# A hybrid decoder layer on one core: what GpSimd did before the MLP goes to VectorE, ScalarE and TensorE

## The chip, the core and the metric

The kernel runs on one core of one Trainium2 chip. The metric is the device time of one execution in microseconds. Five engines work side by side on the core: TensorE (PE in the profile, its weight loads PEld), VectorE (DVE), ScalarE (ACT), GpSimd (POOL) and SyncE (SP), which here only issues the DMAs. Each runs its own instructions in order and waits on semaphores for the others.

## The reference

One layer of a decoder trunk on a residual stream x of 1024 positions by 1024 features, in float32, with a conditioning vector c:

```
mod = silu(c) @ w_mod + b_mod                  # shift, scale, gate for mixer and MLP: 6 x 1024
h = rms(x, norm1_w) * (1 + sc1) + sh1
u, q, k, v = split(h @ w_in)                   # 512 | 512 | 128 | 128
y_ssm  = S5(u): 32 groups of 16 channels, each driving a 64-dim complex diagonal state,
         scan over 1024 positions, y = Re(C s) + D u, z = gelu(y), z * sigmoid(z @ w_glu + b_glu)
y_attn = attention: 8 query heads, 2 key/value heads, window 128, per-head rms of q and k,
         relative bias, sinks
x = x + g1 * (concat(rms(y_ssm), rms(y_attn)) @ w_out)
h2 = rms(x, norm2_w) * (1 + sc2) + sh2
x = x + g2 * ((silu(gate) * val) @ w_down),  [val | gate] = causal_conv3(h2 @ w_up)
```

## The kernel before

Everything lies transposed: features on the 128 partitions, positions along the free dimension, in pieces of 128x512 (half a row of positions, called h = 0 and 1) or 128x1024. Every float32 product is made of three matmuls in a reduced format (`mm3`): each operand is split into a high part, a cast, and a low part, source minus high part (`split`, the cast by `hi_eng`, the subtraction by `lo_eng`). The subtraction and all other two-operand elementwise work goes through the helper `tt(eng, ...)` on line 127, so that VectorE's and GpSimd's share of it have the same line; `cpy` on lines 142 and 144 makes casts and copies. Which engine does which is written in the table `PICK`, one letter for each use (a ScalarE, v VectorE, p GpSimd), read by `pick(name, i)`.

The stages, in order of the program:

1. First projection. For k = 0 to 7 a tile of x (128 features by 1024 positions), a column block of w_mod and half a block of w_in are loaded. `emit_mod` makes one column of mod on VectorE, x times its scale is split into `hT[k]` (hi on ScalarE L261, lo on VectorE), x squared on ScalarE (L265), and the squares are added up in `acc`, by GpSimd from k = 1 on. TensorE adds up the projection U in six banks (j = 0 to 5: every eighth position) as the k come, and j = 6 and 7 beside or after that. From `acc` eight matmuls give the row sums in columns (`rc`, which scales U when it leaves its bank), and two more the sums in rows (`rstd`).
2. Tables. Small VectorE operations on 128x32 (exp, sin, powers `PWr`, `PWi`) give the discretised state matrix; `outer` makes four tiles `IB` and five tiles `CAt` of 128x1024 from them, three elementwise operations each, taken in turn by GpSimd and VectorE.
3. Heads and scan. The order of TensorE's instructions is pinned to the order of the program here. `head(t)` projects k, v and four pairs of q; the SSM inputs `SR` and `SI` are made on TensorE and scanned in twelve steps of `cmac` (six up, six down). Each step multiplies and adds in eight operations on n columns of each of the 16 pairs of groups; the first `SCAN_CUT` of the 16 go to VectorE, with the product in PSUM, the rest to GpSimd.
4. Attention in 16 units (8 blocks of 128 queries, 2 key/value heads), at high priority, beside the SSM's output, GELU and GLU. GpSimd scales most units' softmax by its row sum (`PM`).
5. Norms of the two branches, output projection. For the SSM branch the norm factor `rss` is not in the operand: `proj` multiplies it in when a bank is emptied (VectorE, into `xs_`), and GpSimd adds the result to x (`XA`). For the attention branch VectorE adds straight to x. Sums of squares for the second norm follow (`R`, `RA`).
6. MLP with a seven-product scheme (`product`, `weight`, `took`, `operands`, `mixed`), convolution and down projection. Some of its splits are GpSimd's, before and after the change.

The order on every engine inside a stretch that is not pinned comes from a planner in the framework, which orders the instructions by a model of their times when the program is built. A tag such as X4 or A8 is a buffer; the next use of a tag waits for the last reader. All DMAs are issued from SP's one queue, in order.

Of the kernel before, what the change touches and what calls it, by code (L numbers as in the profile page):

```python
# [27 lines left out]
for _n, _w in (  # L28
# [19 lines left out]
}  # L48

SCAN_CUT = (12, 14, 8, 9, 11, 13, 9, 8, 11, 11, 12, 9)  # L50
# [21 lines left out]
def hymba_kernel(ctx, tc, xT, c, wmod, wu, wkvq, small, consts, relb, pq, wglu, wout, wup, wdn, out):  # L72
# [173 lines left out]
    acc = new("A2")  # L246
    xs = [new("X4"), new("X5"), new("X6"), early[:, 3072:4096]]
    wst = None
    for k in range(8):
        xk = xs[k % 4]  # L250
        sync.dma_start(out=xk, in_=xT[k])
        emit_mod(8 + k, early[:, (k % 3) * 1024:(k % 3 + 1) * 1024], cact)
        if k % 2 == 0:
            wst = new(("W0", "A10")[k // 2 % 2])
            sync.dma_start(out=wst, in_=wu[k // 2])
        w = half(newr(f"U{k}") if k < 4 else wux[:, (k - 4) * 1024:(k - 3) * 1024])
        wus.append(w)
        split(w, wst[:, (k % 2) * 512:(k % 2) * 512 + 512], "a", pick("WL", k))
# [20 lines left out]
    rc = pool.tile([128, 16], F32, name="rc")  # L279
# [139 lines left out]
    tt(pol, gh(Bb), gh(Q1), bg(fr), MUL)  # L419
    tt(pol, gh(jt), gh(Q2), bg(t0), MUL)  # L420
    tt(pol, Bb, Bb, jt, ADD)
    tt(pol, gh(Bsw), gh(Q2), bg(f2), MUL)
    tt(pol, gh(jt), gh(Q1), bg(t2), MUL)
    tt(pol, Bsw, Bsw, jt, ADD)
    tt(pol, P1, P1, S("sgn").to_broadcast([128, 512]), MUL)
    tt(pol, P2, P2, S("neg").to_broadcast([128, 512]), MUL)
# [45 lines left out]
    def head_w(t):  # L472
# [3 lines left out]
        split(w, wst, pick("HWH", t), pick("HWL", t))  # L476
# [195 lines left out]
    sgi = [0]  # L672
    ptmp = CAt[4][:, 576:1024]

    def cmac(l, dst, src, n):
        GP = SCAN_CUT[sgi[0]]
        sgi[0] += 1
        step = max(1, 512 // n)
        cuts = [(vec, g0, min(GP, g0 + step)) for g0 in range(0, GP, step)]
        step = max(1, 448 // n)  # L680
        cuts += [(pol, g0, min(16, g0 + step)) for g0 in range(GP, 16, step)]
        for eng, g0, g1 in cuts:
            shp = [128, g1 - g0, n]
            tp = (bank[7] if eng is vec else ptmp)[:, 0:(g1 - g0) * n].rearrange("p (g c) -> p g c", c=n)
# [19 lines left out]
    for h in range(2):  # L704
        for i in range(4):
            q_ = newr(f"H{8 + 4 * h + i}")
            for kv in range(2):
# [4 lines left out]
                cpy(pick("QH%d" % h, i), q.r[p0, :], src)  # L712
                tt(ENG[pick("QL%d" % h, i)], q.r[p1, :], src, q.f[p0, :], SUB)
# [49 lines left out]
    for h in range(2):  # L763
        for m in range(4):
            zs[m, h] = half(newr(f"A{m + 4 * h}"))
            split(zs[m, h], zT[m][:, h * 512:h * 512 + 512], pick("ZH", m), pick("ZL", m))
    wg = []
    wgt = (newr("HA"), newr("HB"))
    for k in range(4):
# [4 lines left out]
        split(wg[k], wst[:, (k % 2) * 512:(k % 2) * 512 + 512], pick("GH", k), pick("GL", k))  # L774
# [4 lines left out]
    rss = half(new("W1"))  # L779
# [3 lines left out]
    for h in range(2):  # L783
# [8 lines left out]
        acc, sq = half(new(("A8", "A8")[h]))  # L792
        for n in range(4):
            hi, lo = mx[n, h] = half(newr(f"A{n + 4 * h}"))
            src = zT[n][:, hs]
            if pick("MX%d" % h, n) == "a":
                act.activation(out=hi.r, in_=src, func=AF.Identity, scale=bw[:, n:n + 1])
            else:
                ts(hi.r, src, bw[:, n:n + 1], MUL)
            stt(lo.r, src, bw[:, n:n + 1], hi.f, MUL, SUB)  # L800
            if pick("NS0%d" % h, n) == "a":
                act.activation(out=(sq if n else acc), in_=src, func=AF.Square)
            else:
                tt(ENG[pick("NS0%d" % h, n)], (sq if n else acc), src, src, MUL)
            if n:
                tt(ENG[pick("NA0%d" % h, n - 1)], acc, acc, sq, ADD)
        b = sbank()
        pe.matmul(b, ones, acc, start=True, stop=True)
        rsqrt_mean(rss[h], sq, b, 2048)


    def branch_norm(h):
# [4 lines left out]
        for m in range(1, 4):  # L817
            if pick("NS1%d" % h, m - 1) == "a":
                act.activation(out=sq, in_=src[m], func=AF.Square)
            else:  # L820
                tt(ENG[pick("NS1%d" % h, m - 1)], sq, src[m], src[m], MUL)
            tt(ENG[pick("NA1%d" % h, m - 1)], acc, acc, sq, ADD)
# [3 lines left out]
        for m in range(4):  # L826
# [3 lines left out]
            split(mx[4 + m, h], yo, pick("MH1%d" % h, m), pick("ML1%d" % h, m))  # L830
# [65 lines left out]
    def wload(src, lo_eng=None):  # L896
# [5 lines left out]
        split(w, st, pick("LH", i), lo_eng or "p")  # L902
# [6 lines left out]
    def proj(d, h, br_i, b, w):  # L909
# [11 lines left out]
    xs_ = half(new("A8"))  # L921
# [6 lines left out]
    for i, d in enumerate(order):  # L928
        if i % 2 == 0:
# [4 lines left out]
            split(w, st, pick("SH", i // 2), pick("SL", i // 2))  # L934
# [25 lines left out]
    def normed(k, h, rs):  # L960
        t_ = ht[k, h]
        stt(t_, x[k][:, h * 512:h * 512 + 512], mods[:, 8 + k:9 + k], rs, MUL, MUL)
        if pick("HB", 8 * h + k) == "a":
            act.activation(out=t_, in_=t_, func=AF.Identity, bias=mod[:, 24 + k:25 + k])
        else:
            ts(t_, t_, mod[:, 24 + k:25 + k], ADD)
# [55 lines left out]
    def attn_out(d, h):  # L1022
# [4 lines left out]
        if d % 2 == 0:  # L1027
            accs["w"] = wload(wo2[1, :, d:d + 2], pick("AL%d" % h, d // 2))
# [4 lines left out]
        else:  # L1033
            sq = ((sq,) + tuple(spare[h]))[d % 3]
            e_ = pick("R%d" % h, d)
            if e_ == "a":
                act.activation(out=sq, in_=x[d][:, hs], func=AF.Square)
            else:
                tt(ENG[e_], sq, x[d][:, hs], x[d][:, hs], MUL)
            tt(ENG[pick("RA%d" % h, d)], acc, acc, sq, ADD)  # L1040
# [361 lines left out]
```

## Time and profile before

| what | us |
|---|---|
| three runs, median (lowest to highest) | 1176.59 (1175.77 to 1176.9) |
| the profiled execution, its own time | 1173.97 |
| its span, first to last instruction | 1172.2 |

The span is what the views below divide up; the profiled execution's own time is 1.8 us longer. The granted clock of TensorE is 0.949 of full speed over the span. A busy time is the union of the instructions of an engine; neighbours on one engine overlap by some 0.08 us in the records. In the views, an arrow `out<-in` names tiles without their numbers (tX stands for X4 to X7, bk for a PSUM bank, tS for the tile S16). In brackets behind a row is the idle time before it, with what ended it.

### The profile page before, as it was taken

Reading aid. Unit: us, or ns where it says so; the run is one execution under the profiler, and the core shown is the slowest. Engines: PE = TensorE matmul, PEld = TensorE weight load, DVE = VectorE, ACT = ScalarE, POOL = GpSimd, SP = SyncE. Lnnn points to the kernel's source line nnn. Section 1 sums busy time; section 2 is a strip of 40 time slices with the busy share of each in tenths; the row PEclk is TensorE's granted clock in tenths of the full one; section 3 lists DMA queues with packets and bytes.
Section 4 is the critical chain, followed back from the end, with each engine's and each line's share of the span. In section 5 each row is a group of like instructions: output and inputs, shape, how many; then the busy total and the mean of one; then the engine's idle time right before and its main releaser. Section 6 shows DMA issues by size and latency. Waiting matters only on the chain.

```text
span 1172.2 us, 13402 instructions
## 1 busy us (share of the span) xinstructions
PE 1047.8 (89%) x4664; PEld 827.1 (71%) x4664; DVE 997.3 (85%) x1493; ACT 523.9 (45%) x889; POOL 500.7 (43%) x344
## 2 busy tenths in 40 slices
PE   4757989777989788869999999999999979989998
PEld 4646867565656466647888888888888758768777
DVE  8999799988989988698787788878796797997985
ACT  4312232163676234565555454545454455434442
POOL 3674276636266772684222222212122043343551
PEclk9778999978999899889999999999999989999999
DMA  9402330605322633323222333242222439320002
GB/s 355 151 27 72 63 100 19 90 1 146 124 108 106 200 126 123 130 91 107 76 94 101 113 103 114 103 144 73 90 90 72 162 132 406 126 91 1 1 37 107
DMA packets 47334, 128.13 MB, mean 109 GB/s; under 512 B 6017, under 2 KB 13985, under 8 KB 47266
## 3 DMA queue, kind: packets, MB, share of 16 engines
q1 hardware_dynamic: 47266, 127.28, 32.4%
q8 instruction: 36, 0.59, 0.2%
q14 instruction: 32, 0.26, 0.1%
HBM read 105.28 MB, written 21.99 MB: 109 GB/s over the span
## 4 chain that ended last, share of the span: by engine, by line
PE 42%; DVE 11%; DMA 2%; issue 1%; ACT 1%; POOL 0%; SPq 0%; DVEq 0%; POOLq 0%; ACTq 0%
PE bk L106 42%; DVE tA L127 2%; DVE tH L127 2%; DVE tU L127 2%; DMA tX<-in_dram 1%; DVE tX L127 1%; DVE tX L136 1%; DVE tXQ L127 1%; DVE tXQ L136 1%; DMA tS<-in_dram 0%; DVE tHA L127 0%; DVE tW L127 0%; DVE tS L127 0%; DMA tW<-in_dram 0%; DVE tW L136 0%
## 5 line engine op out<-in xcount | busy, mean ns | idle before, releaser
L106 PE MATMUL bk<-tA,tU 128*128 128x512 f32 x516 | 127.7, 394 | 0.8 <-DVE tA L127 0.8
L106 PE MATMUL bk<-tU,tU 128*128 128x512 f32 x516 | 124.0, 392 | 4.8 <-DVE tXQ L136 2.4
L106 PE MATMUL bk<-tH,tU 128*128 128x512 f32 x477 | 117.0, 394 | 0.0
L106 PEld LDWEIGHTS bk<-tU,tU 128*128 128x128 f32 x516 | 97.0, 189 | 27.6 <-issue 2.8
L106 PEld LDWEIGHTS bk<-tA,tU 128*128 128x128 f32 x516 | 96.5, 188 | 24.3 <-DVE tA L127 1.5
L136 DVE SCALAR_TENSOR_TENSOR tX<-tH,sm,tX 128x1023 f32<-128x1023 f32 x66 | 99.3, 1505 | 8.4 <-ACT tX L1137 8.3
L127 POOL TENSOR_TENSOR tU<-tW,tU 128x512 fp32r<-128x512 f32 (+2 forms) x35 | 59.8, 1714 | 108.0 <-ACT tU L142 90.2
L106 PEld LDWEIGHTS bk<-tH,tU 128*128 128x128 f32 x477 | 89.9, 189 | 19.4
L106 PE MATMUL bk<-tXQ,tH 128*128 128x256 f32 (+2 forms) x224 | 58.0, 405 | 19.8 <-ACT tH L261 10.7
L106 PE MATMUL bk<-tA,tXQ 128*128 128x512 f32 x300 | 74.3, 394 | 0.7 <-ACT tH L1090 0.7
L142 ACT CAST tU<-tW 128x512 fp32r<-128x512 f32 (+1 forms) x66 | 46.2, 707 | 54.9 <-DMA tW<-in_dram 19.6
L127 POOL TENSOR_TENSOR tXQ<-tW,tXQ 128x512 fp32r<-128x512 f32 x12 | 48.2, 4024 | 52.0 <-ACT tXQ L142 36.8
L108 PE MATMUL bk<-tH,tU 128*128 128x512 f32 x267 | 65.9, 401 | 4.6 <-DVE tU L127 2.8
L106 PEld LDWEIGHTS bk<-tXQ,tH 128*128 128x128 f32 x224 | 46.7, 262 | 31.7 <-ACT tH L261 12.1
L127 POOL TENSOR_TENSOR tU<-tX,tU 128x512 fp32r<-128x512 f32 x19 | 33.1, 1742 | 83.6 <-ACT tU L142 69.5
L106 PE MATMUL bk<-tH,tA 128*128 128x512 f32 (+1 forms) x168 | 58.8, 500 | 10.3 <-ACT tH L142 4.5
L106 PEld LDWEIGHTS bk<-tA,tXQ 128*128 128x128 f32 x300 | 56.2, 188 | 14.2 <-ACT tH L1090 1.1
L108 PEld LDWEIGHTS bk<-tH,tU 128*128 128x128 f32 x267 | 50.3, 192 | 19.2 <-DVE tU L127 3.6
L127 DVE TENSOR_TENSOR tX<-tX,tX 128x512 f32<-128x512 f32 (+1 forms) x63 | 62.8, 1001 | 1.0 <-DMA tX<-in_dram 0.2
L127 POOL TENSOR_TENSOR tA<-tA,tA 128x1024 f32<-128x1024 f32 (+2 forms) x16 | 39.9, 2494 | 28.4 <-ACT tA L265 18.9
L127 DVE TENSOR_TENSOR tU<-tX,tU 128x512 fp32r<-128x512 f32 x39 | 31.5, 810 | 20.8 <-ACT tU L142 20.7
L106 PEld LDWEIGHTS bk<-tH,tA 128*128 128x128 f32 (+1 forms) x168 | 27.6, 178 | 28.3 <-issue 9.8
(381 smaller groups left out, 2612.4 us busy)
## 6 DMA issues: line engine op xcount, KB each, us to landing
tX<-in_dram SPq DMA_DIRECT2D x51, 512.0 KB, 3.4
tW<-in_dram SPq DMA_DIRECT2D x49, 512.0 KB, 3.4
tS<-in_dram SPq DMA_DIRECT2D x30, 512.0 KB, 4.7
gd<-tX SPq DMA_DIRECT2D x22, 512.0 KB, 2.8
tA<-in_dram SPq DMA_DIRECT2D x12, 512.0 KB, 10.0
tH<-in_dram SPq DMA_DIRECT2D x12, 512.0 KB, 4.8
tH<-gd SPq DMA_DIRECT2D x8, 512.0 KB, 4.7
tA<-gd SPq DMA_DIRECT2D x8, 512.0 KB, 10.1
```

The lines of the kernel that those rows point to most:

```text
L106: return f(*a, **k)
L108: i = f(*a, **k)
L127: return eng.tensor_tensor(out=o, in0=a, in1=b, op=op)
L136: return vec.scalar_tensor_tensor(out=o, in0=a, scalar=s, in1=b, op0=op0, op1=op1)
L142: act.copy(o, i)
```

## The change

Up to the MLP GpSimd keeps the softmax scaling alone (`PM`, 14 of 16 units; 15 before). Everything else that it did there moves:

- splits' low parts (head weights, q, z, GLU weights, branch norms, output weights), the tables `Bb`, `Bsw`, `IB`, `CAt`, the scan, sums of squares of the later norms: to VectorE
- the signs of P1 and P2, squares and casts, and most copies out of PSUM that were VectorE's: to ScalarE
- the sum of squares of the first norm: to TensorE, two matmuls of `ones` with the 128x512 halves of the squares for each k into banks 6 and 7, which j = 6 therefore cannot use inside the loop. `rstd` is made from them before anything leaves the banks, and the eight columns `rc` are taken out of it by eight small matmuls
- the SSM branch's norm factor goes into the operand: each of its eight pieces is multiplied by weight and `rss` and then split; `proj` adds to x in one VectorE operation for both branches, and GpSimd's additions are gone

The MLP is not changed. The core of the diff:

```diff
 PICK = {
-    ... (some 50 entries)
+    "EI": "a", "EK": "a", "EP": "avavavavavavavavavavavavavvaav", "ET": "a", "EU": "avaaavaa", "EV": "a", "EW": "a",
+    "EZ": "av", "NS0": "a", "NS1": "aav", "PM": "pppvppppp", "QH": "a", "ZH": "v", "YB": "67566556",
 }
-SCAN_CUT = (12, 14, 8, 9, 11, 13, 9, 8, 11, 11, 12, 9)
...
-        sq = new(("A11", "A1")[k % 2]) if k else acc
...
-        if k:
-            tt(ENG[pick("XC", k)], acc, acc, sq, ADD)
+        sq = new(("A11", "A1")[k % 2])
+        act.activation(out=sq, in_=xk, func=AF.Square)
...
+        for h in range(2):
+            pe.matmul(bank[6 + h], ones, sq[:, h * 512:h * 512 + 512], start=(k == 0), stop=(k == 7))
...
+    for h in range(2):
+        hs = slice(h * 512, h * 512 + 512)
+        rsqrt_mean(rstd[:, hs], rtmp[:, hs], bank[6 + h], D)
     for j in range(T):
-        pe.matmul(bank[7][:, j:j + 1], acc[:, j:1024:T], ones[:, 0:1], start=True, stop=True)
-    rsqrt_mean(rc[:, 0:8], rc[:, 8:16], bank[7][:, 0:8], D)
+        pe.matmul(bank[7][:, j:j + 1], rstd[0:1, j:1024:T], ones[0:1, 0:1], start=True, stop=True)
+    act.copy(rc, bank[7][:, 0:8])
...
-        pe.matmul(bank[7], ones, acc[:, hs], start=True, stop=True)
-        rsqrt_mean(rstd[:, hs], rtmp[:, hs], bank[7], D)
...
-    tt(pol, gh(Bb), gh(Q1), bg(fr), MUL)          # and five more
-    tt(pol, P1, P1, S("sgn").to_broadcast([128, 512]), MUL)
+    tt(vec, gh(Bb), gh(Q1), bg(fr), MUL)
+    act.activation(out=P1, in_=P1, func=AF.Identity, scale=S("sgn"))
...
-        outer(ENG[pick("IE", i)], IB[i], tmp, 8 * i, 8, 8, Bb, Bsw)
+        outer(vec, IB[i], tmp, 8 * i, 8, 8, Bb, Bsw)
...
-        cuts = [(vec, g0, min(GP, g0 + step)) for g0 in range(0, GP, step)]
-        cuts += [(pol, g0, min(16, g0 + step)) for g0 in range(GP, 16, step)]
+        for g0 in range(0, 16, step):              # all on VectorE, product in bank 7
...
-            hi, lo = mx[n, h] = half(newr(f"A{n + 4 * h}"))
-            act.activation(out=hi.r, in_=src, func=AF.Identity, scale=bw[:, n:n + 1])
-            stt(lo.r, src, bw[:, n:n + 1], hi.f, MUL, SUB)
...
+        for n in range(4):                         # after rsqrt_mean(rss, ...)
+            src = zT[n][:, hs]
+            stt(src, src, bw[:, n:n + 1], rss, MUL, MUL)
+            mx[n, h] = half(newr(f"A{n + 4 * h}"))
+            split(mx[n, h], src)
...
-        if br_i:
-            return stt(x[d][:, hs], b, g1, x[d][:, hs], MUL, ADD)
-        else:
-            stt(st_, b, g1, rss[h], MUL, MUL)
-            return tt(ENG[pick("XA", 2 * d + h)], x[d][:, hs], x[d][:, hs], st_, ADD)
+        return stt(x[d][:, hs], b, g1, x[d][:, hs], MUL, ADD)
```

## Rows read from the trace of the kernel before

**Rows 1.** The page, part 1: busy us, share of the span and instructions by engine.
```profile
PE 1047.8 (89%) x4664; PEld 827.1 (71%) x4664; DVE 997.3 (85%) x1493; ACT 523.9 (45%) x889; POOL 500.7 (43%) x344
```

**Rows 2.** Windows: stretch, its length, busy us (instructions) by engine, granted clock, DMA.
```profile
0.00:110.00 110.00, 74.50 (x256) 63.74 (x256) 102.30 (x187) 32.21 (x42) 59.01 (x30) 0.84 0.45 160
110.00:138.00 28.00, 21.62 (x160) 18.04 (x159) 19.77 (x32) 6.69 (x11) 9.28 (x11) 0.88 0.13 35
138.00:236.00 98.00, 84.82 (x512) 65.70 (x511) 92.66 (x175) 25.98 (x39) 66.09 (x105) 0.97 0.38 74
236.00:400.00 164.00, 141.59 (x669) 99.88 (x670) 147.74 (x328) 96.99 (x242) 91.31 (x55) 0.91 0.32 106
400.00:500.00 100.00, 85.97 (x339) 63.71 (x338) 80.03 (x97) 39.11 (x58) 57.27 (x36) 0.93 0.42 139
500.00:553.00 53.00, 39.93 (x154) 30.91 (x153) 47.74 (x75) 30.26 (x51) 34.32 (x4) 0.84 0.29 95
553.00:1172.00 619.00, 599.39 (x2582) 485.17 (x2580) 507.04 (x604) 292.69 (x448) 183.47 (x106) 0.99 0.29 107
```

**Rows 3.** Waits of TensorE, 0 to 120 us: total, times, longest.
```profile
PE bk L106 <- ACT tH L261: 14.6, 4, 6.4
PE bk L106 <- ACT tHA L261: 12.4, 1, 12.4
PE bk L106 <- DVE tH L136: 8.5, 2, 7.8
PE bk L106 <- DVE brow L484: 6.3, 1, 6.3
```

**Rows 4.** Timeline of GpSimd from 36 us: start, duration, instruction.
```profile
39.38 3.37 POOL L127 TENSOR_TENSOR tA<-tA,tA 128x1024 f32<-128x1024 f32 x1
```

**Rows 5.** Timeline of VectorE, 38 to 52 us, and from 97 us.
```profile
38.03 0.18 DVE L127 TENSOR_TENSOR tU<-tU 128x32 f32<-128x32 f32 x1
...
40.42 2.37 DVE L127 TENSOR_TENSOR tU<-tU 128x32 f32<-128x32 f32 x1
...
51.81 0.69 DVE L127 TENSOR_TENSOR tXQ<-tA,tXQ 128x512 fp32r<-128x512 f32 x1
...
97.62 1.22 DVE L127 TENSOR_TENSOR tA<-Bbt,PWr 128x1024 f32<-128x1024 f32 x1
```

**Rows 6.** Timeline of GpSimd, 495 to 545 us.
```profile
505.02 31.08 POOL L127 TENSOR_TENSOR tXQ<-tW,tXQ 128x512 fp32r<-128x512 f32 x1 [5.36 <-ACT tXQ L142]
```

**Rows 7.** Groups of VectorE by form, before 500 us: busy us, mean ns, idle before.
```profile
L189 DVE CUSTOM_DVE_ANT_0 tS<-tS,sm 128x1024 f32<-128x1024 f32 x16 | 28.8, 1805 | 0.6 <-DMA tS<-in_dram 0.6
...
L136 DVE SCALAR_TENSOR_TENSOR tA<-bk,mod,tW 128x512 f32<-128x512 f32 x16 | 11.7, 742 | 0.7 <-PE bk L106 0.7
L127 DVE TENSOR_TENSOR ep<-ep 128x16 f32<-128x16 f32 x25 | 11.1, 459 | 0.0
...
L127 DVE TENSOR_TENSOR bk<-tS,ep 128x512 f32<-128x512 f32 x4 | 2.8, 701 | 0.3
```

**Rows 8.** Groups of GpSimd by form, whole span.
```profile
L127 POOL TENSOR_TENSOR tU<-tW,tU 128x1024 fp32r<-128x1024 f32 x9 | 22.3, 2480 | 3.2 <-PE bk L106 1.9 <-ACT tU L142 1.2
...
L127 POOL TENSOR_TENSOR tH<-tH,att 128x1024 f32<-128x1024 f32 x8 | 16.8, 2105 | 7.1 <-DVE att L867 5.9 <-PE bk L106 1.1
```

**Rows 9.** Groups of TensorE by form, 0 to 110 us.
```profile
L106 PE MATMUL bk<-tXQ,tH 128*128 128x512 f32 x96 | 33.3, 515 | 18.5 <-ACT tH L261 10.7 <-DVE tH L136 7.8
```

**Rows 10.** Timeline of TensorE, 85 to 122 us.
```profile
94.56 1.81 PE L106 MATMUL bk<-tA,cn 128*128 128x512 f32 x2
...
99.14 3.09 PE L106 MATMUL bk<-tXQ,tH 128*128 128x512 f32 x12
...
102.53 1.02 PE L106 MATMUL bk<-tA,cn 128*128 128x512 f32 x2
...
116.36 0.58 PE L106 MATMUL bk<-cn,brow 2*128 2x1 f32 x2 [6.31 <-DVE brow L484]
```

**Rows 11.** Waits of TensorE, 236 to 500 us, the largest total.
```profile
PE bk L106 <- DVE tA L136: 7.2, 3, 3.5
```

More of the change, by code (lines that the diff above doesn't have):

```diff
@@ L245, in hymba_kernel @@
     jt = new("A12")[:, 0:512]
-    acc = new("A2")
     xs = [new("X4"), new("X5"), new("X6"), early[:, 3072:4096]]
@@ L257, in hymba_kernel @@
         wus.append(w)
-        split(w, wst[:, (k % 2) * 512:(k % 2) * 512 + 512], "a", pick("WL", k))
+        split(w, wst[:, (k % 2) * 512:(k % 2) * 512 + 512])
         stt(mods[:, k:k + 1], mod[:, 8 + k:9 + k], 1.0, n1s[:, k:k + 1], ADD, MUL)
@@ L418, in hymba_kernel @@
     ts(t2, fi, -1.0, MUL)
-    tt(pol, gh(Bb), gh(Q1), bg(fr), MUL)
[L420 to L424, printed above, removed]
-    tt(pol, P1, P1, S("sgn").to_broadcast([128, 512]), MUL)
-    tt(pol, P2, P2, S("neg").to_broadcast([128, 512]), MUL)
+    tt(vec, gh(Bb), gh(Q1), bg(fr), MUL)
+    tt(vec, gh(jt), gh(Q2), bg(t0), MUL)
+    tt(vec, Bb, Bb, jt, ADD)
+    tt(vec, gh(Bsw), gh(Q2), bg(f2), MUL)
+    tt(vec, gh(jt), gh(Q1), bg(t2), MUL)
+    tt(vec, Bsw, Bsw, jt, ADD)
+    act.activation(out=P1, in_=P1, func=AF.Identity, scale=S("sgn"))
+    act.activation(out=P2, in_=P2, func=AF.Identity, scale=S("neg"))
     def outer(eng, o, tmp, g0, ng, nd, u, v):
@@ L475, in head_w @@
         w = (newr(f"U{2 * (t % 2)}"), newr(f"U{2 * (t % 2) + 1}"))
-        split(w, wst, pick("HWH", t), pick("HWL", t))
+        split(w, wst)
         if t >= 2:
@@ L670, in hymba_kernel @@
         tt(vec, ei[l], et, et, ADD)
-    sgi = [0]
-    ptmp = CAt[4][:, 576:1024]
     def cmac(l, dst, src, n):
-        GP = SCAN_CUT[sgi[0]]
-        sgi[0] += 1
         step = max(1, 512 // n)
-        cuts = [(vec, g0, min(GP, g0 + step)) for g0 in range(0, GP, step)]
-        step = max(1, 448 // n)
-        cuts += [(pol, g0, min(16, g0 + step)) for g0 in range(GP, 16, step)]
-        for eng, g0, g1 in cuts:
+        for g0 in range(0, 16, step):
+            g1 = min(16, g0 + step)
             shp = [128, g1 - g0, n]
-            tp = (bank[7] if eng is vec else ptmp)[:, 0:(g1 - g0) * n].rearrange("p (g c) -> p g c", c=n)
+            tp = bank[7][:, 0:(g1 - g0) * n].rearrange("p (g c) -> p g c", c=n)
             e_r = er[l][:, g0:g1].rearrange("p (g o) -> p g o", o=1).to_broadcast(shp)
@@ L765, in hymba_kernel @@
             zs[m, h] = half(newr(f"A{m + 4 * h}"))
-            split(zs[m, h], zT[m][:, h * 512:h * 512 + 512], pick("ZH", m), pick("ZL", m))
+            split(zs[m, h], zT[m][:, h * 512:h * 512 + 512], pick("ZH", m))
     wg = []
@@ L773, in hymba_kernel @@
         wg.append(half(wgt[k // 2][:, (k % 2) * 1024:(k % 2 + 1) * 1024]))
-        split(wg[k], wst[:, (k % 2) * 512:(k % 2) * 512 + 512], pick("GH", k), pick("GL", k))
+        split(wg[k], wst[:, (k % 2) * 512:(k % 2) * 512 + 512])
     mx = {}
@@ L778, in hymba_kernel @@
     ts(bw[:, 4:8], S("ona"), -1.0, MUL)
-    rss = half(new("W1"))
+    rss = new("W1")[:, 0:512]
     sgt = [new("U4"), new("U5")]
@@ L791, in hymba_kernel @@
             stt(zT[n][:, hs], sg, 1.0, zT[n][:, hs], ADD, MUL)
-        acc, sq = half(new(("A8", "A8")[h]))
+        acc, sq = half(new("A8"))
         for n in range(4):
-            hi, lo = mx[n, h] = half(newr(f"A{n + 4 * h}"))
             src = zT[n][:, hs]
-            if pick("MX%d" % h, n) == "a":
-                act.activation(out=hi.r, in_=src, func=AF.Identity, scale=bw[:, n:n + 1])
-            else:
-                ts(hi.r, src, bw[:, n:n + 1], MUL)
-            stt(lo.r, src, bw[:, n:n + 1], hi.f, MUL, SUB)
[L801 to L804, printed above, removed]
+            act.activation(out=(sq if n else acc), in_=src, func=AF.Square)
             if n:
-                tt(ENG[pick("NA0%d" % h, n - 1)], acc, acc, sq, ADD)
+                tt(vec, acc, acc, sq, ADD)
         b = sbank()
         pe.matmul(b, ones, acc, start=True, stop=True)
-        rsqrt_mean(rss[h], sq, b, 2048)
+        rsqrt_mean(rss, sq, b, 2048)
+        for n in range(4):
[3 more added lines that the diff above has]
+            split(mx[n, h], src)
     def branch_norm(h):
@@ L817, in branch_norm @@
         for m in range(1, 4):
[L818 to L822, printed above, removed]
+            act.activation(out=sq, in_=src[m], func=AF.Square)
+            tt(vec, acc, acc, sq, ADD)
         b = bank[(7, 0)[h]]
@@ L829, in branch_norm @@
             mx[4 + m, h] = half(newr(f"H{8 + 4 * h + m}"))
-            split(mx[4 + m, h], yo, pick("MH1%d" % h, m), pick("ML1%d" % h, m))
+            split(mx[4 + m, h], yo)
     hp = ctx.enter_context(ExitStack())
@@ L901, in wload @@
         w = (newr(slots[i][0]), newr(slots[i][1]))
-        split(w, st, pick("LH", i), lo_eng or "p")
+        split(w, st)
         return w
@@ L933, in hymba_kernel @@
             w = (t_[:, 0:1024], t_[:, 1024:2048])
-            split(w, st, pick("SH", i // 2), pick("SL", i // 2))
+            split(w, st)
         wS[d] = w
@@ L962, in normed @@
         stt(t_, x[k][:, h * 512:h * 512 + 512], mods[:, 8 + k:9 + k], rs, MUL, MUL)
[L963 to L966, printed above, removed]
+        act.activation(out=t_, in_=t_, func=AF.Identity, bias=mod[:, 24 + k:25 + k])
     def operand(i, k, v):
@@ L1034, in attn_out @@
             sq = ((sq,) + tuple(spare[h]))[d % 3]
[L1035 to L1040, printed above, removed]
+            act.activation(out=sq, in_=x[d][:, hs], func=AF.Square)
+            tt(vec, acc, acc, sq, ADD)
         return done.ins
```

27 lines of the change are left out of this document (10 added, 17 removed), and 9 rows, old and new, of the table PICK.

## The prediction

> **What bounds the kernel now.** I read the busy times first [rows 1]: TensorE 89% and VectorE 85% of the span, so neither alone explains the time, and the shares must be taken by stage. The windows do that [rows 2]. From 553 us on, in the MLP, TensorE is busy 599.4 of 619 us: that part is bound by TensorE and the change does not touch it. In the 553 us ahead TensorE is idle for 105 us (the six stretches less 74.5, 21.6, 84.8, 141.6, 86.0 and 39.9), while VectorE is busy 102.3 of the first 110 us, 92.7 of 98 and 147.7 of 164. The waits of TensorE in the first 120 us [rows 3] are for operands that VectorE makes, or that ScalarE makes from VectorE's scales (14.6 + 8.5 + 6.3 us; the 12.4 us are the start). So ahead of the MLP VectorE is what TensorE mostly waits for.
>
> Then I ask what VectorE's time is made of. A 128x32 operation took 0.18 us at 38.03 and 2.37 us at 40.42 [rows 5]; GpSimd's 3.37 us addition ran from 39.38 to 42.75 [rows 4], and VectorE's ended at 42.79 with it. So the small operation did not work for 2.37 us, it stood behind GpSimd's. The 25 operations on 128x16 (ep) took 0.459 us in the mean [rows 7]. The reverse is there too: in the run of two-operand VectorE work from 505 us one GpSimd subtraction lasted 31.08 us [rows 6], against 1.24 if half of a 128x1024 one's 2.48 is taken [rows 8]. VectorE and GpSimd take turns. Taking every form of VectorE's instructions at its quickest twentieth, the 815 that start before 498 us sum to 368 us instead of 491: about 122 us are time behind GpSimd.
>
> The row of VectorE reading a PSUM bank has a mean of 0.742 us over 16, stretched little if at all [rows 7]. The Trainium skill, "SBUF — State Buffer", section "Who interferes with whom", has the rule: an exclusive lock on a shared port pair for the whole instruction, which concerns VectorE instructions with two SBUF inputs or in a two-port mode. The trace agrees.
>
> **The change by parts.** Durations of one operation: VectorE 0.69 us for 128x512 and 1.22 for 128x1024 [rows 5], GpSimd 2.48 for 128x1024 [rows 8].
>
> VectorE gains, counted in the diff: 25 operations of 1024 columns (IB 6, CAt 6, head weights 5, output weights 3 + 4, one scaling) at 1.22 = 30.5 us; 54 of 512 (Bb 6, q 8, z 8, GLU weights 3, operand scaling 8, branch norms 13, second norm 8) at 0.69 = 37.3; six of 288 at 0.4 (scaled from 0.69) = 2.4; and GpSimd's share of the scan. There 16 minus SCAN_CUT times n, summed over the twelve steps, is 1236 columns, times 8 operations, at 0.701 us per 512 [rows 7] = 13.5 us; no additional instructions, since the groups join cuts that exist. Sum 84 us. VectorE loses 36 copies, casts and squares to ScalarE (EU 1, EI 4, EK 1, EV 2, EZ 4, ET 7, QH 8, weights' and norms' 5, squares 4) of 0.4 to 0.7 us: 19 us. Net +65.
>
> It loses the standing behind GpSimd: 122 us, less what the 14 scalings left do, at most 14 x 2.1 = 29 us [rows 8]; I take half, 15. So VectorE's 442.5 busy us before 500 [rows 2] become 442.5 + 65 - 122 + 15 = 400. ScalarE takes some 20 us on 201 us in the same 500 [rows 2]; TensorE and GpSimd's idle time hide nothing of that, but ScalarE is under 60% busy everywhere.
>
> What that is worth, by stage:
>
> First projection, to the end of the j = 7 matmuls at 102.2 us [rows 10], and the wait for brow behind it, 6.3 [rows 3]: 108.5. After: TensorE starts at 12.4 as now [rows 3], has the same 192 matmuls, 16 sums of two records each, and then waits for rstd. The matmul costs 0.258 us at the fastest (3.09/12 [rows 10]) and 0.347 in the mean of the stage (33.3/96 [rows 9]); a sum 1.02 to 1.81 us [rows 10], one per granted clock. The chain behind the last sum (two ScalarE and two VectorE operations, the second half one behind the other) is about six of 0.69 = 4.1 us (estimate), in which j = 6 cannot begin, since it needs bank 6. Lowest: 12.4 + 49.4 + 16.3 + 4.1 = 82.2, saving 26. Highest: 12.4 + 66.6 + 29.0 + 4.1 + 6 for a quarter of the waits of 23.1 = 118, losing 9.5. VectorE's and the loads' part of one k (scale, low part, weight split, some 3.2 us) is under TensorE's 6 to 9, so TensorE sets it and runs without breaks; I take 0.30 and 1.25 per instruction: 12.4 + 57.6 + 20 + 4.1 + 2 = 96. With brow ready in time (the tables are done by then): -12.5.
>
> Heads and scan, 110 to 236: TensorE busy 106.4, idle 19.6 with brow's 6.3, so 13 can be had. VectorE 112.4 [rows 2], of which GpSimd's 75.4 us of scan and splits stretch about a quarter; with 13.5 of scan and some 5 of splits added, 7 of copies gone, about 95. Then TensorE's pinned order is nearer to being the bound. I take -7; bounds -13 and +5 (the scan is one dependent chain, and every head's result queues behind it on VectorE).
>
> Attention and GLU, 236 to 400: TensorE idle 22.4 [rows 2]; VectorE 147.7 becomes some 140, since the scalings stay and about 17 us net is added. Behind the norm, the SSM operands now come three operations later than the GLU's sums, some 2 us, beside attention. -6; bounds -15 and +6.
>
> Branch norms and output projection, 400 to 500: TensorE idle 14.0 [rows 2], with waits on VectorE as the largest [rows 11]; the 16 additions of GpSimd are gone with no VectorE time in their place, 10 us added otherwise. -5; bounds -12 and +5.
>
> From 500: nothing, +-3.
>
> Sum: -12.5 - 7 - 6 - 5 = -30.5. The profiled execution's 1173.97 becomes 1143.5; its median of three runs lies 2.6 us above that profile, so 1146.
>
> A rule speaks against the change: the Trainium skill, "Perfetto Trace Analysis", section "Optimizing Scalar/DVE Operations", says that with VectorE saturated offloading to ScalarE or even GpSimd may make sense; the same paragraph doubts it between VectorE and GpSimd, which share a read port. By the first half VectorE's +65 us would stand on a full engine; rows 4 and 5 show the second half at work. It is rival E below.
>
> **Rivals.**
>
> A. Faster, but TensorE takes VectorE's place in the first stage: 16 sums and the chain eat the stage's gain, with -2 left, and half of the other stages' 18 comes. 2.6 + 1173.97 - 11 = 1166. For it: the sums are new work on the busiest engine. Against: 23 us of waits there.
>
> B. Slower: the first stage's clock. The stretch 0 to 110 has a granted clock of 0.84 [rows 2], between the levels of 1.2 and 2.4 GHz, and TensorE waited for operands in it. If it stays low, sums of 1.81 and matmuls of 0.347 give the +9.5 worked out above, and the other stages, with VectorE serial in the scan, at their slow bounds halved give +8: 1176.6 + 17 = 1194 at worst, 1186 in the middle. It decides when the sums cost over 1.6 us each and the other stages gain under 8 us. Against: the waits that let the clock fall are the ones removed.
>
> C. No change: the planner's new order puts VectorE's additional work ahead of what TensorE waits for, and gives back what the lock took: 1176.
>
> E. VectorE is full, and GpSimd's share was a real relief: nothing comes off for standing behind GpSimd, and 442.5 + 65 = 507.5 us of work at VectorE's present share of 88% (442.5 of 500) need 573 us: slower by 73, 1250. It needs the stretched rows to have another cause; that VectorE's ended 0.04 us after GpSimd's [rows 4, 5] speaks against it.
>
> D. More: every stage near its fast bound, -26 - 13 - 10 - 8: 1120.
>
> **How the numbers follow.** Forecast 0.58 (its own range 1132 to 1158), A 0.18, D 0.05, C 0.05, B 0.12, E 0.02. From 1176.59, 0.2% is 2.4 us, about what a measurement can tell from no change. Faster: forecast, A and D, 0.80 with a little off for A's upper end; same 0.06; slower 0.14. The range 1116 to 1182 leaves out most of B, E and the end of D.
>
> **What would show it.** Right: VectorE's 128x32 operations near 0.18 us throughout the first 110 us; its busy time before the MLP down by some 40 us though it has more instructions; brow's wait gone; the j = 7 matmuls ending near 96 us; the MLP's 619 us as they are. Wrong: VectorE's mean durations unchanged; sums at 1.8 us with TensorE busy without a break and still past 102 us; the MLP starting no earlier than 553.

## The result: 3% faster, and the profile after

The changed kernel takes 1140.24 us (median of four runs, 1137.94 to 1142.15) against 1176.18 (1175.33 to 1176.9) for the kernel before, beside it on the same chip: ratio 0.9694, 95% interval 0.9671 to 0.9716. The profiled execution took 1142.15 us, its span 1140.29. That is 31.9 us less than the profiled span of before; the median moved by 35.9.

First the page's part 1 of the changed kernel, which answers to [rows 1]:

```profile
PE 1053.4 (92%) x4692; PEld 828.2 (73%) x4692; DVE 957.5 (84%) x1541; ACT 550.2 (48%) x936; POOL 256.7 (23%) x137
```

VectorE has 48 instructions more and is busy for 39.8 us less; GpSimd's busy time has halved. Why VectorE's does not grow is to be read from the operations that the change left alone. Two rows of VectorE's timeline of the changed kernel (start, duration, instruction), the same kind of operation as in [rows 5]:

```profile
28.60 0.20 DVE L118 TENSOR_TENSOR tU<-PWi,tU 128x32 f32<-128x32 f32 x1
...
30.89 0.18 DVE L118 TENSOR_TENSOR tU<-tU 128x32 f32<-128x32 f32 x1
```

No 128x32 operation of 2 us is left. The 25 operations on `ep`, 459 ns in the mean in [rows 7], show it as a group (changed kernel, VectorE by form, before 467 us):

```profile
L118 DVE TENSOR_TENSOR ep<-ep 128x16 f32<-128x16 f32 x25 | 3.8, 169 | 0.2
```

Where the time came from is read at the same instructions of TensorE in both traces. The changed kernel's timeline of TensorE, at the end of the j = 7 matmuls, at the first brow matmul (`brow` is a head's bias row, copied out of a PSUM bank by VectorE; both in [rows 10]), at the first matmul of the attention, at the last block of 24 of the output projection's first branch, and at the first product behind the second norm:

```profile
85.12 3.44 PE L97 MATMUL bk<-tXQ,tH 128*128 128x512 f32 x12
...
96.28 0.38 PE L97 MATMUL bk<-cn,brow 2*128 2x1 f32 x2 [0.76 <-DVE brow L471]
...
207.74 1.74 PE L97 MATMUL bk<-tXQ,tH 128*128 128x128 f32 x4
...
424.26 6.19 PE L99 MATMUL bk<-tA,tHA 128*128 128x512 f32 x24
...
453.15 0.73 PE L99 MATMUL bk<-tS,tU 128*128 128x512 f32 x2 [0.95 <-ACT tU L133]
```

and the last three in the kernel before:

```profile
237.49 1.74 PE L106 MATMUL bk<-tXQ,tH 128*128 128x128 f32 x4
...
452.28 6.15 PE L108 MATMUL bk<-tA,tHA 128*128 128x512 f32 x24
...
485.56 1.22 PE L108 MATMUL bk<-tS,tU 128*128 128x512 f32 x2 [2.41 <-ACT tU L142]
```

The differences of neighbouring rows give a table by stage:

| stage | before | after | gain | forecast |
|---|---|---|---|---|
| to the first brow matmul | 116.36 | 96.28 | -20.1 | -12.5 |
| heads and scan, to the first attention matmul | 121.13 | 111.46 | -9.7 | -7 |
| attention and GLU, to the block of 24 | 214.79 | 216.52 | +1.7 | -6 |
| block of 24 to the second norm's first product | 33.28 | 28.89 | -4.4 | -5 |
| the rest of the span | 686.6 | 687.1 | +0.5 | 0 |

The forecast divided the third stage from the fourth at 400 us, earlier than the table does; together the two were to gain 11 us and gained 2.7. The first two stages gained more than forecast, the last did not move; the attention gave nothing. The experiments have two questions: is it really GpSimd's presence that cost VectorE its time, and what holds the attention back?

### The profile page after: what moved, and what is told of

Its sections match the earlier page's. It is cut to its first block, busy times and chain, and to the rows that moved or that the text cites. A ratio compares the mean times of both kernels' runs of the same rounds, so it can differ in the third digit from the quotient of the medians.

```text
span 1140.3 us, 13281 instructions
## 1 busy us (share of the span) xinstructions
PE 1053.4 (92%) x4692; PEld 828.2 (73%) x4692; DVE 957.5 (84%) x1541; ACT 550.2 (48%) x936; POOL 256.7 (23%) x137
## 4 chain that ended last, share of the span: by engine, by line
PE 60%; DVE 29%; ACT 4%; DMA 3%; issue 3%; POOL 1%; SPq 0%; ACTq 0%; DVEq 0%; POOLq 0%
PE bk L97 54%; PE bk L99 6%; DVE tA L118 5%; DVE tU L118 3%; DVE tH L118 3%; DVE tS L118 2%; DVE tX L127 2%; DMA tW<-in_dram 2%; DVE bk L118 2%; DVE tS L180 1%; DVE tXQ L118 1%; DVE tXQ L127 1%; DVE tX L118 1%; DVE tX L180 1%; ACT tU L133 1%
## 5 line engine op out<-in xcount | busy, mean ns | idle before, releaser
L97 PE MATMUL bk<-tH,tU 128*128 128x512 f32 x477 | 116.0, 392 | 0.0
L118 POOL TENSOR_TENSOR tU<-tW,tU 128x512 fp32r<-128x512 f32 x25 | 36.3, 1462 | 174.1 <-ACT tU L133 152.4
L97 PE MATMUL bk<-tH,tA 128*128 128x512 f32 (+1 forms) x168 | 63.9, 509 | 11.4 <-ACT tH L133 7.6
L99 PE MATMUL bk<-tH,tU 128*128 128x512 f32 x267 | 64.0, 395 | 1.8 <-DVE tU L118 1.7
L118 POOL TENSOR_TENSOR tH<-tH,att 128x1024 f32<-128x1024 f32 (+1 forms) x9 | 19.1, 2124 | 195.8 <-DVE att L840 161.7
L118 POOL TENSOR_TENSOR tXQ<-tW,tXQ 128x512 fp32r<-128x512 f32 x12 | 49.1, 4102 | 53.1 <-ACT tXQ L133 37.8
L97 PE MATMUL bk<-tXQ,tH 128*128 128x256 f32 (+2 forms) x224 | 51.9, 374 | 4.3 <-DVE att L828 4.3
L118 DVE TENSOR_TENSOR tU<-tW,tU 128x512 fp32r<-128x512 f32 (+2 forms) x43 | 37.8, 881 | 20.4 <-ACT tU L133 20.4
```

Source lines behind the costliest of these rows:

```text
L97: return f(*a, **k)
L99: i = f(*a, **k)
L118: return eng.tensor_tensor(out=o, in0=a, in1=b, op=op)
```

## Experiments

All runs are compared with runs of the kernel before on the same chip.

**One part alone: tables.** In the kernel before:

```diff
-    "CE": "pv", ... "IE": "pv"
+    "CE": "v", ... "IE": "v"
-    tt(pol, gh(Bb), gh(Q1), bg(fr), MUL)        # and five more, outer(pol, CAt[4], ...)
+    tt(vec, gh(Bb), gh(Q1), bg(fr), MUL)
-    tt(pol, P1, P1, S("sgn").to_broadcast([128, 512]), MUL)      # and P2
+    act.activation(out=P1, in_=P1, func=AF.Identity, scale=S("sgn"))
```

> The kernel before, with one part of the change alone: the tables (Bb, Bsw, IB, CAt) all on VectorE, their two sign scalings on ScalarE. Theory (VectorE stood behind GpSimd's long instructions, whoever does the work): some 25 us of work come onto VectorE in the first 140 us and yet TensorE's j = 7 matmuls end earlier than 102.2 us, at 94 to 98, because the small 128x32 operations go back to about 0.2 us; total -5 to -12 us, ratio 0.990 to 0.996. Rival (GpSimd's share was a relief and the gain comes from the copies given to ScalarE or the new order of the sums): the end of j = 7 is at 102 or later, brow's wait grows, total 0 to +15 us.

1164.93 us, ratio 0.9927 (0.9904 to 0.9949): the theory's total, with the j = 7 matmuls even earlier. TensorE in this kernel:

```profile
83.79 3.11 PE L106 MATMUL bk<-tXQ,tH 128*128 128x512 f32 x12
...
106.02 0.58 PE L106 MATMUL bk<-cn,brow 2*128 2x1 f32 x2 [0.20 <-DVE brow L484]
```

VectorE took over the work and j = 7 ended 15.3 us earlier, at 86.90. Part of that is lost again: the brow matmul comes 10.3 us earlier only, since VectorE, without a pause (19.12 of the 19.12 us between the two), still makes tables.

**One part alone: the first norm's sums on TensorE.** In the kernel before:

```diff
-        if k:
-            tt(ENG[pick("XC", k)], acc, acc, sq, ADD)
+        for h in range(2):
+            pe.matmul(bank[6 + h], ones, sq[:, h * 512:h * 512 + 512], start=(k == 0), stop=(k == 7))
...
-        pe.matmul(bank[7], ones, acc[:, hs], start=True, stop=True)      # behind j = 6 and 7
-        rsqrt_mean(rstd[:, hs], rtmp[:, hs], bank[7], D)
```

> The kernel before, with one part alone: the first norm's sums of squares made by TensorE (16 sums over the eight k) in place of GpSimd's seven additions and the two sums behind j = 6 and 7. Theory (turn-taking): seven additions of some 3.4 us fewer for VectorE to stand behind, but 14 more sums of about 1 us on TensorE: end of j = 7 at 99 to 103 us, total -4 to +3 us, ratio 0.997 to 1.003; tables on GpSimd still stretch the rest. Rival (the sums are what brought the first stage's 20 us): end of j = 7 below 93 us, total -10 us or more.

1166.45 us, 0.9929 (0.9904 to 0.9954): theory and rival both missed the total (-8.1 us). The end of j = 7 stayed at 102.42 us as the theory had it, but the brow matmul moved to 109.67, because the sum and the scale chain behind j = 7 are gone, and with them the wait of 6.31 us in [rows 10] (0.29 now). I had counted the part's cost and forgotten that tail.

**Both.**

> The kernel before with both parts of the first stage: tables off GpSimd and the first norm's sums on TensorE. Alone the tables moved the end of j = 7 from 102.2 to 86.9 us but the first brow matmul only from 116.4 to 106.0; the sums left j = 7 at 102.4 and moved brow's matmul to 109.7. Theory (two different places, the tables VectorE's standing behind GpSimd ahead of j = 7, the sums the two sums and scale chains behind it): they add, brow's matmul at 97 to 101 us, total -15 to -20 us against the kernel before, ratio 0.983 to 0.987. Rival (they are two ways out of one wait): brow's matmul at 104 or later, total -8 to -12 us.

1151.79 us, 0.9802 (0.9788 to 0.9817). Brow's matmul came at 95.67 and the total fell by 22.8 us, both a little beyond the theory's range: the two add up and more (-9.7 and -8.1 alone). Where the 5 us beyond their sum come from was not taken apart. This is the whole first stage of the change (96.28).

**The scan alone, on VectorE.** `SCAN_CUT = (16,) * 12` in the kernel before.

> The kernel before, with the scan alone all on VectorE: 13.5 us of work more for VectorE in one dependent chain, and 8 to 10 us per step of GpSimd gone beside it. Theory (turn-taking): the scan's VectorE operations and those of the heads between them come back to their bare time, which pays for the added work and a little more; last head matmul 232.8 us becomes 226 to 231, total -2 to -7 us. Rival (the division of the scan between two engines was a gain in itself): the chain is longer by about 13 us, TensorE waits for the heads' results, total +4 to +13 us.

1181.4 us, 1.0062 (1.0046 to 1.0079). The theory was right on the stage, the last head matmul at 228.81 instead of 232.80, and wrong on the total, which is the rival's. The last operation of the scan, in VectorE's timeline of the kernel before and of this one:

```profile
231.03 0.22 DVE L127 TENSOR_TENSOR tS<-tS,bk 128x63 f32<-128x63 f32 x1
```

```profile
250.68 0.67 DVE L127 TENSOR_TENSOR tS<-tS,bk 128x504 f32<-128x504 f32 x1
```

The heads, in whose order TensorE runs here, were a little quicker; the scan itself ended 20 us later, as VectorE now does all of its steps beside the work for the heads. I had looked at the heads alone. But the later end does not explain the 6.8 us: the GLU's first matmul came at 275.16 us, only 0.5 later than before (row below), because 43.4 us lay between the scan's end and the GLU in the kernel before and 23.8 here. The second norm's first product came at 491.72, 6.2 us later. So the loss is made behind the GLU's start, and it is no larger than what a neutral new order costs below (6.6 us): this run does not show that the scan caused it. TensorE in the kernel before:

```profile
274.63 0.51 PE L106 MATMUL bk<-tA,tHA 128*128 128x512 f32 x1 [0.54 <-DVE tA L144]
```

**The change without tables, scan and sums.** These three as before, all else changed.

> The changed kernel with three parts undone: tables, scan share and first norm's sums as in the kernel before; the splits' low parts, the copies on ScalarE, the norms' additions and the branch norm's fold stay changed. Theory: the first stage gives back most of its 20 us and the scan some more, the gain behind 400 us stays: 1156 to 1168 us, ratio against the kernel before 0.983 to 0.993. Rival (casts on ScalarE, low parts and order of issue carry the gain): 1140 to 1148 us, ratio under 0.977. Second rival (the three parts are all of it): 1174 or more.

1160.06 us, 0.9882 (0.9864 to 0.9899), as the theory had it.

**GpSimd's presence by itself.** The changed kernel, with two additions in each k that nothing reads:

```diff
+    idle = new("A2")
+    pol.memset(idle, 0.0)
...
+        tt(pol, idle, idle, sq, ADD)
+        tt(pol, idle[:, 0:512], idle[:, 0:512], idle[:, 512:1024], ADD)
         for h in range(2):
             pe.matmul(bank[6 + h], ones, sq[:, h * 512:h * 512 + 512], start=(k == 0), stop=(k == 7))
```

> The changed kernel with two additions by GpSimd in each k of the first projection, 128x1024 and 128x512, on a scratch tile that nothing reads: 16 instructions, some 2.5 and 1.2 us each, about 30 us of GpSimd. No engine waits for their results; only a later table tile uses their buffer. Theory (taking turns): VectorE's operations that fall beside them stretch to GpSimd's whole instruction, VectorE's busy time in 0 to 110 us grows by 8 us or more with the same work, the end of j = 7 moves from 88.6 to 93 to 100 us, total +4 to +12 us. Rival (GpSimd's work does not touch the others; the gain came from where the work was put): j = 7 within 1.5 us of 88.6, total within 2 us of 1140.

1164.23 us, 0.9906 (0.9891 to 0.9921): 24 us slower than the changed kernel, twice the theory's upper end and more than the whole gain of the first stage. The window from the start to the end of j = 7, first in the changed kernel, then with the additions (columns as in [rows 2]):

```profile
0.00:88.55 88.55, 72.22 (x241) 60.97 (x242) 81.56 (x198) 32.34 (x42) 0.21 (x4) 0.92 0.51 195
```

```profile
0.00:113.02 113.02, 78.03 (x241) 62.21 (x242) 106.77 (x198) 31.99 (x42) 40.00 (x21) 0.88 0.42 152
```

The same 198 instructions of VectorE, 25.2 us longer; 40.0 us of GpSimd beside them; the end 24.5 us later. No wait of another engine in this window ends on a GpSimd instruction, so it is not a dependence. Summed operation by operation from the two traces, 22.2 us of the lengthening fall on VectorE's operations with two inputs in SBUF, 3.2 on its 24 `TENSOR_SCALAR` of 128x32, and nothing on the four that read a PSUM bank. One place, GpSimd and then VectorE:

```profile
32.04 3.13 POOL L118 TENSOR_TENSOR tA<-tA,tA 128x1024 f32<-128x1024 f32 x1 [3.78 <-ACT tU L362]
35.25 2.15 POOL L118 TENSOR_TENSOR tA<-tA 128x512 f32<-128x512 f32 x1
```

```profile
32.86 3.40 DVE L180 CUSTOM_DVE_ANT_0 tA<-tA,tX,sm 128x1024 f32<-128x1024 f32 x1
36.19 0.08 DVE L180 DVE_READ_ACCUMULATOR2_ANT mod<- 128x1 f32 x1
36.19 1.29 DVE L118 TENSOR_TENSOR PWr<-tU 128x32 f32<-128x32 f32 x1
```

The mod column, 1.27 us in the changed kernel at 38.38, took 3.40, most of them behind GpSimd, and the 128x32 operation ended at 37.48, with GpSimd's (35.25 + 2.15 = 37.40). TensorE then waits for ScalarE and VectorE (four waits of 10.3 us in all for `tH`, and more), as in [rows 3].

**The changed kernel with the scan divided again** (`SCAN_CUT` and its two kinds of cuts back).

> The changed kernel with the scan alone divided again between VectorE and GpSimd as in the kernel before. Theory (the scan stage is quicker on VectorE, what was lost in the earlier run with the scan alone came later and from another order of the attention): the stretch from the first brow matmul to the first QK matmul (111.5 us) grows by 2 to 4 us, and the total moves by -3 to +5 us. Rival (the whole share on VectorE costs time in the attention as well, by whatever way): the stretch from the first QK matmul to the first product of the second norm's inputs (245.4 us) shrinks by 4 us or more and the total is 1132 to 1137 us, ratio against the kernel before under 0.967.

1126.28 us, 0.9585 (0.9566 to 0.9603): 14 us better than the changed kernel, more than the rival had. The scan's last operation in the changed kernel and here:

```profile
229.28 0.67 DVE L118 TENSOR_TENSOR tS<-tS,bk 128x504 f32<-128x504 f32 x1
```

```profile
201.68 0.22 DVE L120 TENSOR_TENSOR tS<-tS,bk 128x63 f32<-128x63 f32 x1
```

The attention begins at the same time in both (207.74 and 207.45 us). But the scan ends 28 us earlier, 5.6 us ahead of the attention as in the kernel before (231.25 to 237.49: 6.2), and not 22.2 behind its start. What follows on it is the GLU, whose first matmul, in TensorE's timeline in the same order, comes 12.9 us earlier:

```profile
257.09 2.11 PE L97 MATMUL bk<-tA,tHA 128*128 128x512 f32 x8
```

```profile
244.15 1.00 PE L99 MATMUL bk<-tA,tHA 128*128 128x512 f32 x2 [0.48 <-DVE tA L137]
```

The stretch from the first attention matmul to the end of the block of 24, again in this order (columns as in [rows 2]):

```profile
207.74:430.44 222.70, 194.74 (x869) 137.57 (x868) 191.21 (x426) 129.70 (x292) 29.98 (x14) 0.90 0.36 123
```

```profile
207.45:413.71 206.26, 186.82 (x867) 128.97 (x866) 184.37 (x415) 124.99 (x289) 31.55 (x14) 0.96 0.38 130
```

It is 16.4 us shorter: 8.5 us less idle time of TensorE (27.96 and 19.44), and 7.9 less busy time for the same matmuls, at a granted clock of 0.96 instead of 0.90.

How far does GpSimd's part stretch VectorE's? VectorE by form, 130 to 230 us, all on VectorE first, then divided:

```profile
L127 DVE SCALAR_TENSOR_TENSOR tX<-tX,tX 128x512 f32<-128x512 f32 x10 | 6.8, 678 | 0.0
...
L118 DVE TENSOR_TENSOR bk<-tS,ep 128x504 f32<-128x504 f32 x8 | 5.5, 684 | 0.1
L118 DVE TENSOR_TENSOR tS<-tS,bk 128x504 f32<-128x504 f32 x8 | 5.4, 675 | 0.1
```

```profile
L129 DVE SCALAR_TENSOR_TENSOR tX<-tX,tX 128x512 f32<-128x512 f32 x10 | 8.6, 868 | 0.0
...
L120 DVE TENSOR_TENSOR bk<-tS,ep 128x504 f32<-128x504 f32 x4 | 3.2, 795 | 0.0
...
L120 DVE TENSOR_TENSOR tS<-tS,bk 128x504 f32<-128x504 f32 x4 | 2.7, 672 | 0.1
```

Operations with both operands in SBUF are stretched (678 to 868 ns, 684 to 795); the one that takes an operand from a PSUM bank is not (675, 672). Half of the scan's operations are of that kind, and over the stage VectorE is no busier than without GpSimd (97.88 us of 112.32, against 98.32 of 111.46). The Trainium skill, "SBUF — State Buffer", section "Who interferes with whom", says that a VectorE instruction with at most one SBUF input, outside the two-port modes, does not contend with GpSimd; these rows agree.

**Is that the planner's order?** The planner orders anew with every edit. Two edits that change no work: VectorE's softmax scalings given in other units (`PM`), in the kernel before and in the changed one.

```diff
-    "PM": "pppvpppppppppppp"
+    "PM": "ppppppvppppppppp"
...
-    "PM": "pppvppppp"
+    "PM": "ppppppvpp"
```

> The kernel before with the one softmax scaling that VectorE makes given in unit 6 in place of unit 3: no work is added or taken away, but the planner orders part of the attention anew. Theory (what the planner's order does by chance is small against the effects told): total within 2.4 us of the kernel before, ratio 0.998 to 1.002. Rival (a new order of the attention alone moves the time by as much as the scan's edit did): 4 us or more to either side.

1181.1 us, 1.0048 (1.0031 to 1.0065): slower by 6.6 us without any work added, as the rival had it. Most of it is one wait, between the block of 24 and the second norm; TensorE of this kernel, and the cast that it waits for on ScalarE:

```profile
471.97 19.79 PE L108 MATMUL bk<-tH,tU 128*128 128x512 f32 x72 [7.86 <-ACT tU L142]
```

```profile
470.87 1.04 ACT L142 CAST tU<-tW 128x1024 fp32r<-128x1024 f32 x1 [1.22 <-DMA tW<-in_dram]
```

In this order the weight's load lands late. In the changed kernel:

> The changed kernel with VectorE's two softmax scalings given in units 6 and 15 in place of 3 and 12; the work is the same and the planner orders part of the attention anew. The same kind of edit moved the kernel before by +6.6 us, and dividing the scan again moved the changed kernel by -14 us, of which 5 us are there when the scan ends. Theory (the other 9 us are the order of the attention, which a neutral edit moves as well): the total moves by 4 us or more to either side, and all of it between the first QK matmul and the MLP. Rival (the 9 us belong to the scan's division itself): within 3 us of 1140.

1141.4 us, 0.9707 (0.9682 to 0.9732): no change beyond 2 us, as the rival had it. So an order can cost 6 us, and need not. The 14 us of the divided scan are more than either, and 12.9 of them are there at the GLU's first matmul. That place holds under other orders too: with the scan on VectorE the GLU starts at 257.09, 255.15 (this run) and 257.56 us (the next one), with the scan divided at 244.15, 244.79 and 244.04 (the two last runs). What a new order did besides was not taken apart: each edit of the scan changes both.

**The copies back on VectorE** (`EI`, `EK`, `EV`, `EZ`, `ET`, one of `EU`, in the changed kernel).

> The changed kernel with the copies out of PSUM (EI, EK, EV, EZ, ET and one of EU) back on VectorE as in the kernel before: some 16 copies of 0.4 to 0.7 us, 10 us of VectorE's work ahead of the MLP. Theory (turn-taking carries the gain, these copies are a small relief of VectorE): +2 to +8 us, and the first stage unchanged, j = 7 at 88 to 90 us. Rival (the copies on ScalarE carry a large part of the gain): +15 us or more. By the order's chance alone up to 6 us to either side.

1142.06 us, 0.972 (0.9701 to 0.9739): slower by 1.8 us by the medians and 3 by the ratios, in the theory's range. The copies do not carry the gain.

**All softmax scalings on VectorE**, scan divided (`"PM": "v"`).

> The changed kernel with the scan divided again (1126.3 us) and in addition all 16 softmax scalings on VectorE, so that GpSimd does nothing from the scan to the MLP. Theory by the forecast's sizes (14 scalings cost up to 29 us of standing behind and would cost 17 us as VectorE's own work): VectorE's busy time in 240 to 500 us falls by up to 10 us, total -8 to +2 us. Rival (GpSimd's scalings lie beside VectorE's work at little cost): VectorE's busy time grows, total +3 to +12 us.

1136.03 us, 0.9667 (0.9648 to 0.9687): the rival's total, not its reason. The block of 24 ends at 414.89 us instead of 413.71, and the first attention matmul came 1.3 us later too, so the 14 scalings between them cost nothing; VectorE's busy time between these two points fell from 184.37 to 180.90 us, in the theory's direction. The loss is one wait behind them:

```profile
421.35 24.50 PE L101 MATMUL bk<-tH,tU 128*128 128x512 f32 x94 [5.75 <-DVE tU L120]
449.04 1.22 PE L101 MATMUL bk<-tS,tU 128*128 128x512 f32 x2 [3.18 <-ACT tU L135]
```

A weight's low part stands behind the second norm's operations on VectorE, by the order; the clock then is lower as well (granted 0.84 from the end of the block of 24 to the second norm's first product, against 1.00; the 94 matmuls take 24.50 us, 96 took 21.93 in the kernel without this edit).

**The MLP's splits off GpSimd too**, scan divided:

```diff
-        split(w, {...}[i], "a", "p" if i in (1, 2, 4) else "v")
+        split(w, {...}[i], "a", "v")
-        split(r_, v, "a", "vvp"[cn_["split"] % 3])
+        split(r_, v, "a", "v")
```

> The changed kernel with the scan divided again (1126.3 us) and in addition all splits of the MLP on VectorE, which GpSimd shared before and after (179 us of it in the MLP). Theory: the MLP is bound by TensorE, which is busy 598 of 617 us there, so at most some 15 us can come; by turn-taking VectorE's 504 us change little, as it loses standing behind and gains the work: total -6 to +4 us. Rival (in the MLP GpSimd's share is a true relief, VectorE becomes the bound): TensorE's waits for VectorE grow, total +10 us or more.

1118.43 us, 0.9516 (0.9495 to 0.9537), the fastest of all and 7.9 us under the kernel without this edit, a little more than the theory had. From the second norm's first product to the end, with GpSimd's share and without:

```profile
436.82:1122.37 685.55, 652.12 (x2774) 524.87 (x2774) 561.38 (x684) 327.04 (x507) 222.44 (x115) 0.98 0.29 105
```

```profile
436.26:1116.43 680.17, 652.20 (x2774) 526.39 (x2774) 561.88 (x801) 326.42 (x507) 0.00 (x0) 0.98 0.29 107
```

222.44 us of GpSimd are gone, VectorE does 117 instructions more, and its busy time is the same within 0.5 us. GpSimd relieved it of nothing. Here TensorE sets the time (busy 652 us in both), so only 5.4 us came in this stretch of the profiled executions.

## Why the prediction was right, and where it was not

The forecast was 1146 us (own range 1132 to 1158); 1140.24 came.

**The cause** held. VectorE's busy time up to the MLP was to fall by 42.5 us with more instructions; up to the MLP (its first `bk<-tA,tXQ` matmul, at 542.14 us before and 504.86 after) it fell from 482.00 us over 878 instructions to 440.57 over 924, by 41.4 (columns as in [rows 2]; before, then after):

```profile
0.00:542.14 542.14, 437.57 (x2036) 333.13 (x2037) 482.00 (x878) 224.96 (x432) 315.74 (x237) 0.90 0.37 114
```

```profile
0.00:504.86 504.86, 438.09 (x2064) 331.35 (x2065) 440.57 (x924) 252.23 (x479) 74.62 (x30) 0.92 0.38 121
```

TensorE is busy as long as before, 437.57 and 438.09 us, and idle for 37.8 us less. The terms hold too, and not the sum alone. Taken as the prediction took them, each form at its quickest twentieth, VectorE's instructions in these two stretches need 410 of their 537 us (durations added up) before and 467 of 497 after: the work grew by 57 us (65 forecast), the excess, which the prediction puts down to standing behind GpSimd, shrank from 127 to some 29 (15 forecast to be left). Rival E is gone: useless work on GpSimd, which takes nothing off VectorE, cost 24 us, and taking real work off GpSimd in the MLP left VectorE as busy as it was. Rival B as well: in the first 110 us the clock rose from 0.84 [rows 2] to 0.94, and the sums' 32 instructions took 16.9 us, 1.06 for each pair of records. A went the other way: TensorE does stand in VectorE's place there (busy without a break from 10.6 to 61.5 us, VectorE for 50.5 of these 50.9 us beside it) and the stage still gained most.

**First stage**, -12.5 forecast, -20.1 came. The term mis-sized is TensorE's busy time: 57.6 + 20 = 77.6 us, and 72.22 came, eight small matmuls of 4.0 us included that I had left out. The single terms were close (192 matmuls at 0.307, from groups of 58.9 us in all, against 0.30; sums 16.9 against 20), but added up the groups make 79.8: neighbouring records overlap by some 0.16 us, and where two groups alternate, the sum counts that twice. Of the 7.5 us by which j = 7 ended ahead of the forecast 96, this is 5.4; the start is 1.8 (10.6 us instead of 12.4, as a sum comes first). Brow's wait went as forecast, from 6.31 to 0.76 us.

**Heads and scan**, -7 forecast, -9.7 came, and the scan has little part in it: divided again, the stage takes 112.3 us instead of 111.5; alone on VectorE in the kernel before it took 118.4 (116.65 to 235.05) instead of 121.1. The rest is from tables, sums and the other changes, each of which alone made it 119.7 us (tables: 106.02 to the first attention matmul at 225.68), 118.3 (sums: 109.67 to 228.00) and 118.1 (the rest: 114.61 to 232.73) instead of 121.1.

**Attention and GLU**, -6 forecast, +1.7 came, within the bounds (-15 and +6). The step that failed is the scan's. I had named the chain and its queue on VectorE as a bound of the heads' stage (+5), charged 13.5 us, took the standing behind GpSimd off in return, and ended the stage with the last head. But the scan does not end with the heads: on VectorE alone it ended 22 us into the attention, and the GLU started 49.4 us behind the first attention matmul (257.09 - 207.74) where it had been 37.1 (274.63 - 237.49). From the scan's end to the GLU it was 43.4 us before and 27.1 here: the slack is used up and the rest shows as delay. With the scan divided it is 36.7 from the attention's first matmul, and the stretch gains 14.7 us on before (206.26 against 220.94; this is the row of before):

```profile
237.49:458.43 220.94, 192.01 (x869) 136.51 (x868) 197.67 (x389) 112.84 (x263) 122.91 (x73) 0.92 0.36 119
```

That the forecast total was so close is luck: the first two stages gained 10.3 us more than forecast, the attention 7.7 less.

**Rival C**, the planner's order, was put at "no change" for the whole. It is a term of its own: 6.6 us in the one reordering of two that moved the time.

**From 500 us** 0 was forecast, and the last stage moved by 0.5. That too is two parts that offset each other: from the second norm's first product to the MLP's first matmul 51.7 us instead of 56.6, from there to the end 635.4 instead of 630.1, beyond the forecast's 3 us. In the MLP the same matmuls are busy for 5.0 us more (615.29 and 610.25); the cause of that is open. The 31.08 us subtraction of [rows 6] is still there:

```profile
469.29 31.15 POOL L118 TENSOR_TENSOR tXQ<-tW,tXQ 128x512 fp32r<-128x512 f32 x1 [5.30 <-ACT tXQ L133]
```

## What to carry to other kernels

Before giving GpSimd a part of VectorE's work, look in the trace for short VectorE operations that end together with a GpSimd one: where VectorE's operations read two operands from SBUF, the two engines took turns here, and the relief was nothing or less. A dependent chain can be another matter: in the changed kernel the scan, with half of its operations on PSUM, was worth dividing, because its end came late enough to move the start of the next stage. In the kernel before, with 43 us between the two, a scan that ended 20 us later moved the GLU by 0.5. With a planner in between, run a neutral reordering once before a few microseconds are explained.

## What the runs showed that was not expected

- In the first stage 40.0 us of GpSimd's operations cost VectorE 25.2 us and the kernel 24. The two overlapped for 39.2 us, but GpSimd's operations are stretched as well (2.35 to 3.99 us for 128x1024, 1.26 to 2.30 for 128x512); each at its quickest, the sixteen would need 8 x 2.35 + 8 x 1.26 = 28.9 us (estimate), and the price is close to that.
- From the second norm on, VectorE's busy time did not depend on who did the work: 561.38 us with 684 instructions and GpSimd busy for 222.44, 561.88 with 801 and GpSimd idle.
- A GpSimd operation of 128x512 was held for 31.15 us while VectorE ran some fifty two-operand operations of 0.67 us one behind the other. Taking turns was not even: VectorE, which did not pause in these 31 us, kept GpSimd out.
